# Grouped-query scores with the low part of the keys on both halves of the partitions

## The chip, the cores and the metric

The kernel runs on one core of a Trainium2 chip. The metric is the time of one execution on the device in microseconds (us), taken as the median of several runs. The engines that matter here are TensorE (PE in the rows; PEld is its weight load), VectorE (DVE), ScalarE (ACT) and GpSimd (POOL).

## The reference

Two transformer layers over 512 latent tokens and 256 context tokens, width 1024, then a third block of another kind. In each layer there is, between two feed-forward halves, a mix of three parts: neighbourhood attention, pooling, and grouped-query attention with 8 query heads over 2 key heads of width 64. The change is in the scores of the last one:

```python
def _gqa_attend(q, k, v):
    s = jnp.einsum('bqkgd,bskd->bkgqs', q, k, preferred_element_type=jnp.float32) * (q.shape[-1] ** -0.5)
    p = jax.nn.softmax(s, axis=-1).astype(v.dtype)
    return jnp.einsum('bkgqs,bskd->bqkgd', p, v)
```

The latent queries attend to all 768 keys in both layers; the context queries attend to the 256 context keys, in layer 0 alone.

## The kernel before

Products are made from split operands. A float32 value is kept as a high part in the short float format (F32R) and a low part, the rest. `mm3` (L279 to L284) adds three matmuls for each pair of blocks: high by high, high by low, low by high; most of the kernel's time is spent there.

Scores of the grouped queries are stacked instead. A head has 64 rows, half of the 128 partitions. `stack_q` (L557) puts the high part of one head's queries on one half and the low part on the other; GpSimd's DMA queue carries the low part across (L564, L565). `QS` holds eight such stacks. `KS` (L590) has three slots of 768 keys. Slots 0 and 1 hold the high part of key head 0 and 1, and `other_half` (L649 to L651) copies each to the other half of the partitions, so that one matmul of 128 rows gives high by high and low by high. Slot 2 holds the low parts, head 0 on the lower half and head 1 on the upper (L623), and a second matmul of 64 rows adds high by low.

`scores` (L567) makes these two matmuls (L571 and L572) for each PSUM bank. A latent task (`gqa_tasks`, L756) is 128 queries of two heads: for each head 512 and 256 keys, so four matmuls a head. There are 16 tasks in each layer. A context task (`ctx_tasks`, L785) has one bank of 256 keys for each head, two heads a task, eight such tasks in layer 0, and then four more for the other attention (L802).

A task runs through `soft` (L508): the maximum on VectorE (L513), the exponential on ScalarE (L515), the reciprocal and the scaling on VectorE (L502, L506). Then `pair_pv` (L477) transposes the probabilities three or four chunks at a time on TensorE (L487), evacuates each group to SBUF, three on ScalarE and one on VectorE in turn (L491, L493), and multiplies by the values (L497, a form of 128 rows by 64 columns). `pipeline` (L528) emits the scores of a task and its softmax ahead of the previous task's product. There are two PSUM buffers for scores and three for transposes. The order on each engine is then set before the launch by a planner that works with estimated times; each engine runs its queue in that order. When the last reader of `QS` and `KS` is done, their space goes to the values of the neighbourhood attention, which GpSimd's queue then loads (L709), followed there by the pooling.

The lines before the change:

```python
            self.nc.tensor.matmul(S[:, c:c + n], q, kl[0][:, k], start=True, stop=False)
            self.nc.tensor.matmul(S[:, c:c + n], q[h], kl[1][h, k], start=False, stop=True)
```

Of the kernel before, what the change touches and what calls it, by code (L numbers as in the profile page):

```python
# [10 lines left out]
F32 = mybir.dt.float32  # L11
# [17 lines left out]
# columns of the small-vector array  # L29
# [16 lines left out]
class Net:  # L46
# [9 lines left out]
    # ------------------------------------------------------------------ set-up  # L56
    def setup(self):
# [20 lines left out]
        # conditioning vectors as stationary operands, padded to 32 columns  # L78
# [6 lines left out]
        # column i of ones  # L85
# [11 lines left out]
    def weights(self, src, pool=None, ahead=AHEAD, eng=None):  # L97
        """A [128, 1024] piece of weights, split."""
        pool = pool or self.W
        with self.tc.high_priority(offset=ahead):  # L100
            raw = self.raw()
            self.nc.sync.dma_start(raw, src)
            W = tuple(pool.tile([128, 1024], F32R, name=f"w{x}", tag=f"w{x}", bufs=4 if pool is self.W else 2) for x in "hl")
            self.split(*W, raw, eng)
        return W

    def unit(self, src, pool=None):
        """256 columns of a weight, as (hi, lo) per 128 rows."""
        W = []
        for q in range(2):  # L110
            w = [x.rearrange("p (k c) -> p k c", k=4) for x in self.weights(src[:, 1024 * q:1024 * q + 1024], pool)]
            W += [tuple(x[:, k] for x in w) for k in range(4)]
        return W

    # ------------------------------------------------------------------ conditioning
    def ada(self, n):
        """Chunk n of the modulation: 0-17 for the two layers, 18-20 for the last block."""
# [10 lines left out]
        for k in range(KB):  # L128
            raw = self.fp.tile([128, 1024], F32, name="rawf", tag="rawf", bufs=self.nraw)
            nc.sync.dma_start(raw, src[:, k])  # L130
            if acc:
                # the sums over rows 128 apart on the vector engine, those over the partitions at the end
# [36 lines left out]
    def open_psum(self):  # L169
        """The PSUM banks of all phases but attention: transposes and sums, products, modulation."""  # L170
# [9 lines left out]
    def fill_chunk(self):  # L180
        """Finish the chunk that fill has begun, so that its PSUM bank is free."""
# [3 lines left out]
    def fill(self, n=1):  # L185
        """Emit n steps of the work that waits for nothing in the main chain."""
# [7 lines left out]
    # ------------------------------------------------------------------ norms  # L194
# [6 lines left out]
    def parts(self, ctx):  # L201
        """The pieces in which one phase hands the tokens over to the next: (column of the modulation, first, number)."""
# [13 lines left out]
    def rstd_rows(self, src, c0, n, eps):  # L216
        """PSUM bank with (mean(src)+eps)^-0.5 of each column, on all partitions."""
# [26 lines left out]
    def norm_mod(self, l, i, part):  # L244
        """aT = rmsnorm(h) * norm_g * (1 + scale) + shift of some tokens, split for the float32r products."""
# [19 lines left out]
    def defer(self, fn, depth=2):  # L265
        """Emit fn after the next depth deferred ones, so that the tensor engine has products to do until its input is there."""
# [12 lines left out]
    def mm3(self, ps, w, a, first, last):  # L279
        """ps += w^T a with both operands split in two parts."""  # L280
# [5 lines left out]
    # ------------------------------------------------------------------ feed-forward  # L286
    def ffn(self, l, i, up, down, ctx, hand_over, beside=None):
        """h += gate / 2 * swiglu(aT); hand_over(part) is called as soon as a part of h is final."""
# [8 lines left out]
        with ExitStack() as es:  # L297
# [48 lines left out]
            for n in splits[:-1]:  # L346
                us, wd = [], []
                for f in range(f0, f0 + n):
                    if f == 0 and not beside:
                        # the norm of the last part runs on beside the first two blocks of the others  # L350
# [11 lines left out]
                    # not at the ends, where the norms need the vector engine  # L362
# [11 lines left out]
                    if dp is not None:  # L374
                        if f < 2:
                            # the last of the norms comes first
# [20 lines left out]
    # ------------------------------------------------------------------ attention and pooling  # L397
    def na_bias_scratch(self, l):
        """The relative bias laid out by query column, row distance and key column, in DRAM."""
# [24 lines left out]
    def rope_tables(self, l):  # L424
        """[q, k] x token tile x [cos, +-sin] tables with the norm gain (and 1/8 for q) in them."""
# [16 lines left out]
    def head_norm(self, ps, nh, t, which, out):  # L442
        """out = rope(rmsnorm(ps) * g) for the heads of one token tile (no rotation for the context)."""
# [25 lines left out]
    def transpose_to(self, src, n, ev):  # L469
        """PE transposes of n chunks of 128 columns; ev takes the PSUM bank."""  # L470
# [6 lines left out]
    def pair_pv(self, P, n, v, o):  # L477
        """o = [V_a^T P_a^T; V_b^T P_b^T] of two heads, for n key chunks of 128."""
# [29 lines left out]
    def soft(self, S, n, act=False):  # L508
        """The softmax of the rows of S."""
# [9 lines left out]
    def follow(self, tasks, fn):  # L519
        """Let fn be called after the last of the tasks."""  # L520
# [7 lines left out]
    def pipeline(self, tasks, depth, beside=iter(()), steps=(), deep=None):  # L528
        """Each task is (scores, softmax, product, after): the scores and the softmax run ahead of the product.

        The scores of the tasks from deep on run two tasks ahead. beside is other work, in steps, for the tensor engine to
        do meanwhile.
        """
# [23 lines left out]
    def stack_q(self, dst, a, b, src):  # L557
        """Two heads on the two halves of the partitions: [hi; lo] stacks of the first (dst a) and [lo; hi] of the second."""
# [8 lines left out]
    def scores(self, S, q, ks, kl, h):  # L567
        """S[128 queries, keys] from stacked operands, in banks: (column, key slice) pairs."""
        for c, k in ks:
            n = k.stop - k.start  # L570
            self.nc.tensor.matmul(S[:, c:c + n], q, kl[0][:, k], start=True, stop=False)  # L571
            self.nc.tensor.matmul(S[:, c:c + n], q[h], kl[1][h, k], start=False, stop=True)  # L572

    def mix(self, l, qctx, hand_over):
# [5 lines left out]
        with ExitStack() as es, ExitStack() as fs, ExitStack() as rs:  # L580
# [9 lines left out]
            KS = qk.tile([128, 3, NT], F32R, name="KS")  # L590
            nc.gpsimd.memset(U, 0.0)
            with ExitStack() as ws:
# [20 lines left out]
                def ev_kv(t, p):  # L613
# [5 lines left out]
                    def ev(pt):  # L619
                        for b in range(2):  # L620
                            h = slice(64 * b, 64 * b + 64)
                            nc.scalar.activation(KS[h, b, ts], pt[h, :128], AF.Copy)
                            nc.vector.tensor_tensor(KS[h, 2, ts], pt[h, :128], KS[h, b, ts].bitcast(F32), OP.subtract)  # L623
# [25 lines left out]
                def other_half():  # L649
                    for b in range(2):  # L650
                        nc.gpsimd.dma_start(KS[64 - 64 * b:128 - 64 * b, b], KS[64 * b:64 * b + 64, b])  # L651
# [17 lines left out]
                def ev_u(b, p, nm, c0, n):  # L669
                    u0 = 8 if nm == "x" else 536  # L670
                    done = nc.scalar.activation(U[:, b, u0:u0 + n], p, AF.Copy)
                    if b == 0 and c0 == 0:
                        # the table of the exponential, ahead of the attention
# [8 lines left out]
            with ExitStack() as ats:  # L682
                self.ges.close()
                if not qctx:
                    # from here on token t = 4 i + r is at place 128 r + i
# [37 lines left out]
            # output projection: the first blocks of all tokens, then the last ones part after part  # L723
# [28 lines left out]
    def places(self, x, perm):  # L752
        """Columns in the order of the tokens when token 4 i + r is at place 128 r + i."""
        return x.rearrange("d (r i) -> d i r", r=4) if perm else x

    def gqa_tasks(self, QS, KS, vc, oT, perm):  # L756
        """Grouped-query attention of the latent tokens over all tokens, heads (i, 4 + i) at a time."""
        tasks = []
        for i in range(4):
            st = {}  # L760
            for t in range(4):
# [3 lines left out]
                def scores(i=i, ts=ts, d=d):  # L765
                    d["S"] = []
                    for b in range(2):
                        S = self.ps.tile([128, 1024], F32, name="S", tag="s")
                        self.scores(S, QS[:, 2 * i + b, ts], [(0, slice(0, 512)), (512, slice(512, NT))], (KS[:, b], KS[:, 2]),
                                    slice(64 * b, 64 * b + 64))  # L770
# [14 lines left out]
    def ctx_tasks(self, QS, KS, vc, qaT, kaT, va, oT):  # L785
        """Both attentions of the context over itself, two heads at a time."""
        mm = self.nc.tensor.matmul
        tasks = []
        for i in range(6):
            st = {}  # L790
            for t in range(2):
# [3 lines left out]
                def scores(i=i, ts=ts, d=d):  # L795
                    S = self.ps.tile([128, 1024], F32, name="S", tag="s")
                    for b in range(2):
                        r = slice(64 * b, 64 * b + 64)
                        if i < 4:
                            self.scores(S, QS[:, 2 * i + b, ts], [(512 * b, slice(NX, NT))], (KS[:, b], KS[:, 2]), r)  # L800
# [20 lines left out]
    def na_tasks(self, qaT, kaT, va, vj, nab, oT, perm):  # L821
        """Neighbourhood attention: 16 columns of all rows, two heads at a time."""
# [51 lines left out]
    def pool_mix(self, l, U, oT, qctx, ap):  # L874
        """Windowed means minus the input, a product per group, and the scale."""
# [28 lines left out]
    # ------------------------------------------------------------------ last block: Hyena filters  # L904
# [3 lines left out]
    def split_tables(self):  # L908
        """The cos and sin tables of both directions, split, to DRAM."""
# [9 lines left out]
    def dft_tables(self, pool, which):  # L919
        """cos and sin tables of one direction, split: [128, 2 (cos, sin), 1024] each."""  # L920
# [6 lines left out]
    def dft_forward(self, ps, tab, z, cs, par, kb):  # L927
        """ps = the cos or sin sums over the tokens of one parity, for 128 frequencies."""
# [4 lines left out]
    def sine(self, out, ps, b, f, pool):  # L933
        """out = sin(f * (ps + b)), the argument taken to [-pi, pi] first."""
# [11 lines left out]
    def filters(self):  # L946
        """Spectra of the two long filters, scaled for the inverse, to DRAM.

        The even part of a filter pair (forward + backward) gives the cosine sums, the odd part the sine sums.
        """  # L950
# [5 lines left out]
        with ExitStack() as es:  # L956
# [17 lines left out]
            # the backward filter has no tap at 0  # L974
# [4 lines left out]
            for cs in range(2):  # L979
# [5 lines left out]
                for hf in range(2):  # L985
# [3 lines left out]
                    for o in range(2):  # L989
# [7 lines left out]
                        for par in range(2):  # L997
# [6 lines left out]
                            if par == 0 and cs == 0:  # L1004
# [3 lines left out]
                                # frequency 256  # L1008
# [29 lines left out]
    # ------------------------------------------------------------------ last block  # L1038
# [3 lines left out]
    def b2_block(self, W, evs, cols=slice(0, NX)):  # L1042
        """The two feature-major blocks of a unit, each given to its ev."""
# [14 lines left out]
    def block2_norm(self, part):  # L1058
        """The final norm of h and the modulated layer norm of that, of the tokens at some places.

        h becomes hg = h * final_g less its mean; the final norm is r (h + mean) with r in rr[.., 0], r * mean in rr[.., 1].
        """
# [7 lines left out]
        # the mean of hg, on all partitions  # L1070
# [20 lines left out]
        # per token, tokens on partitions: the sum of h^2 and the mean of hg  # L1091
# [12 lines left out]
        # s = r (r^2 var + eps)^-0.5  # L1104
# [24 lines left out]
    def residual(self):  # L1129
        """The final norm of h times 2^(1/4), tokens on partitions, to DRAM."""  # L1130
# [139 lines left out]
    def b2_rattn(self, sr):  # L1270
        """sigmoid(r_attn); four of the blocks take the place of the queries and keys that are done."""
# [13 lines left out]
    def b2_merge_attn(self, sr):  # L1285
        """sigmoid(r_attn) * (y_attn @ w_proj_attn), to DRAM."""
# [12 lines left out]
    def proj(self, s, q):  # L1299
        """Four blocks of one of the two merge projections, split."""  # L1300
# [6 lines left out]
    def b2_hyena(self):  # L1307
        """Input projections of the Hyena branch and its two long convolutions; the gates fill the tensor engine meanwhile."""
# [316 lines left out]
def arrays_of(i):  # L1625
    c = np.ascontiguousarray
    A = {}
# [133 lines left out]
```

## Time and profile before

| what | value |
|---|---|
| median of 3 runs | 3518.68 us (3505.75 to 3519.12) |
| span of the profiled execution, first to last instruction | 3509.3 us |
| TensorE busy | 3429.8 us, 98% of the span |
| VectorE, ScalarE, GpSimd busy | 57%, 32%, 10% |
| granted TensorE clock, mean | 0.986 of full speed |
| latent scores and products, layer 0 | 786.9 to about 886 us |
| latent scores and products, layer 1 | 2270.8 to about 2376 us |

The profile gives the span of the profiled execution, not its time with what lies around it; the span is 9.4 us under the median of the runs. Times within the trace count from the first instruction. A matmul's end is modelled, and matmuls overlap, so the pace of TensorE is read from the starts of consecutive matmuls. [...]

### The profile page before, as it was taken

To read this page: it belongs to the slowest core of one execution; us is meant where nothing else is said; L and a number is where in the kernel's file an instruction comes from. 1 tells how busy PE (TensorE), PEld (TensorE's weight loads), DVE (VectorE), ACT (ScalarE), POOL (GpSimd) and SP (SyncE) were. 2 spreads that over 40 slices of the span, in tenths; PEclk is the share of its full clock that TensorE was granted. 3 is DMA by queue.
4 is the path that set the end of the run, shared out by engine and by line. 5 is a ranking of instruction groups with operands and counts; after the bars stand their busy time and mean duration, and the time that the engine had idled before them with its cause. 6 is when DMAs were issued, how large, how long until landed. Compare 5 with 4: busy or idle time off the path is not lost.

```text
span 3509.3 us, 51702 instructions
## 1 busy us (share of the span) xinstructions
PE 3429.8 (98%) x21236; PEld 2937.4 (84%) x21236; DVE 1990.6 (57%) x3373; ACT 1107.3 (32%) x2008; POOL 366.1 (10%) x432
## 2 busy tenths in 40 slices
PE   7999999999899999999999999999999999999997
PEld 5888889996599888899888889866888897777886
DVE  7535566835754566566455447467644463343687
ACT  4311112425632212223111123445422243344331
POOL 3300000231200000000000001512000010000134
PEclk9999999999999999999999999999999999999999
DMA  7533343131122344422344441302323223122344
GB/s 265 165 108 108 108 132 115 50 75 16 24 85 72 111 130 133 129 75 97 97 150 144 133 137 34 94 7 87 111 96 103 72 89 106 62 70 97 127 172 148
DMA packets 112861, 362.75 MB, mean 103 GB/s; under 512 B 15751, under 2 KB 25547, under 8 KB 111984
## 3 DMA queue, kind: packets, MB, share of 16 engines
q1 hardware_dynamic: 90208, 307.59, 27.0%
q0 software_dynamic: 22416, 51.85, 5.1%
q8 instruction: 167, 2.74, 0.3%
q14 instruction: 70, 0.57, 0.1%
HBM read 338.12 MB, written 19.31 MB: 102 GB/s over the span
## 4 chain that ended last, share of the span: by engine, by line
PE 67%; DVE 4%; ACT 1%; DMA 1%; issue 1%; POOL 0%; DVEq 0%; ACTq 0%; POOLq 0%
PE mm L282 16%; PE mm L283 16%; PE mm L284 16%; PE pw L282 3%; PE pw L283 3%; PE pw L284 3%; PE ops L497 2%; PE ptr L487 2%; PE S L572 1%; PE S L1236 1%; PE S L571 1%; DMA rawf<-in_w_ada 0%; DVE P L506 0%; DVE raw L1473 0%; DVE s L855 0%
## 5 line engine op out<-in xcount | busy, mean ns | idle before, releaser
L283 PE MATMUL mm<-aTl,wh 128*128 128x256 f32 (+1 forms) x2992 | 988.6, 331 | 0.0
L282 PE MATMUL mm<-aTh,wh 128*128 128x256 f32 (+1 forms) x2992 | 985.5, 331 | 2.3 <-ACT aTh L259 2.3
L284 PE MATMUL mm<-aTh,wl 128*128 128x256 f32 (+1 forms) x2992 | 986.8, 330 | 0.0
L283 PEld LDWEIGHTS mm<-aTl,wh 128*128 128x128 f32 x2992 | 569.3, 190 | 57.1 <-issue 4.1
L282 PEld LDWEIGHTS mm<-aTh,wh 128*128 128x128 f32 x2992 | 568.6, 191 | 56.7 <-ACT aTh L259 3.2
L284 PEld LDWEIGHTS mm<-aTh,wl 128*128 128x128 f32 x2992 | 569.6, 190 | 53.7 <-issue 2.9
L277 DVE TENSOR_TENSOR wl<-raw,wh 128x1024 fp32r<-128x1024 f32 x292 | 357.9, 1227 | 346.8 <-ACT wh L276 342.4
L276 ACT ACTIVATE wh<-raw 128x1024 fp32r<-128x1024 f32 x300 | 317.1, 1059 | 454.3 <-PE mm L283 287.4
L282 PE MATMUL mm<-uh,dh 128*128 128x256 f32 (+1 forms) x1368 | 449.8, 329 | 3.1 <-DVE h L340 1.9
L283 PE MATMUL mm<-ul,dh 128*128 128x256 f32 (+1 forms) x1368 | 448.3, 328 | 0.0
L284 PE MATMUL mm<-uh,dl 128*128 128x256 f32 (+1 forms) x1368 | 448.2, 328 | 0.0
L340 DVE SCALAR_TENSOR_TENSOR h<-mm,hg,h 128x256 f32<-128x256 f32 (+1 forms) x512 | 292.2, 582 | 174.9 <-PE mm L284 174.3
L319 DVE TENSOR_TENSOR sil<-sil,mm 128x256 f32<-128x256 f32 (+1 forms) x170 | 90.5, 533 | 342.6 <-PE mm L284 340.2
L282 PEld LDWEIGHTS mm<-uh,dh 128*128 128x128 f32 x1368 | 260.3, 190 | 28.0 <-DVE h L340 2.7
L283 PEld LDWEIGHTS mm<-ul,dh 128*128 128x128 f32 x1368 | 260.3, 190 | 22.8 <-issue 0.8
L284 PEld LDWEIGHTS mm<-uh,dl 128*128 128x128 f32 x1368 | 260.3, 190 | 22.7 <-issue 0.4
L135 DVE SCALAR_TENSOR_TENSOR acc<-rawf,cond,acc 128x1024 f32<-128x1024 f32 x189 | 236.0, 1281 | 72.4 <-DMA rawf<-in_w_ada 71.7
L276 ACT ACTIVATE dh<-rawf 128x1024 fp32r<-128x1024 f32 x88 | 92.0, 1058 | 489.1 <-DMA rawf<-in_ffn_down 376.1
L318 ACT ACTIVATE sil<-mm 128x256 f32<-128x256 f32 (+1 forms) x170 | 78.9, 464 | 457.9 <-PE mm L284 456.8
L277 DVE TENSOR_TENSOR dl<-rawf,dh 128x1024 fp32r<-128x1024 f32 x88 | 107.1, 1223 | 104.9 <-ACT dh L276 104.5
L282 PE MATMUL pw<-aTh,wh 128*128 128x512 f32 x400 | 158.6, 396 | 1.1 <-ACT x L1343 1.1
L283 PE MATMUL pw<-aTl,wh 128*128 128x512 f32 x400 | 157.9, 395 | 0.0
(389 smaller groups left out, 4994.5 us busy)
## 6 DMA issues: line engine op xcount, KB each, us to landing
raw<-in_ffn_up SPq DMA_DIRECT2D x176, 512.0 KB, 3.8
rawf<-in_w_ada SPq DMA_DIRECT2D x168, 512.0 KB, 4.4
raw<-in_w_in SPq DMA_DIRECT2D x100, 512.0 KB, 3.6
rawf<-in_ffn_down SPq DMA_DIRECT2D x88, 512.0 KB, 3.6
raw<-in_w_out SPq DMA_DIRECT2D x24, 512.0 KB, 5.4
Hs<-Hf POOLq DMA_DIRECT2D x16, 256.0 KB, 3.6
dft<-tab POOLq DMA_DIRECT2D x8, 512.0 KB, 6.2
raw<-in_w_proj SPq DMA_DIRECT2D x8, 512.0 KB, 3.7
```

The costliest lines, as they stand in the source:

```text
L135: nc.vector.scalar_tensor_tensor(acc[i], raw, self.cond[:, k, x:x + 1], acc[i], op0=OP.mult, op1=OP.add)
L276: self.hi = self.nc.scalar.activation(hi, src, AF.Copy)
L277: return (eng or self.nc.vector).tensor_tensor(lo, src, hi.bitcast(F32), OP.subtract)
L282: mm(ps, w[0], a[0], start=first, stop=False)
L283: mm(ps, w[0], a[1], start=False, stop=False)
L284: mm(ps, w[1], a[0], start=False, stop=last)
L318: nc.scalar.activation(s[:, :n], ps[0][:, :n], AF.Silu)
L319: nc.vector.tensor_tensor(s[:, :n], s[:, :n], ps[1][:, :n], OP.mult)
L340: nc.vector.scalar_tensor_tensor(self.h[:, j, c0:c0 + n], p[:, :n], hg[0][:, j, v:v + 1], self.h[:, j, c0:c0 + n], op0=OP.mult, op1=OP.add)
L487: nc.tensor.transpose(pt[:, 128 * c:128 * c + 128], P[b][:, 128 * (c0 + c):128 * (c0 + c) + 128], self.ident)
L497: nc.tensor.matmul(o[64 * b:64 * b + 64], v(b, c), PT[b][c], start=c == 0, stop=c == n - 1)
L571: self.nc.tensor.matmul(S[:, c:c + n], q, kl[0][:, k], start=True, stop=False)
```

## The change

`KS` gets a fourth slot. The low part of key head 1 goes to slot 3 instead of sharing slot 2, and `other_half` carries the slots b and 2 + b across together, so that each low part too stands on both halves. The second matmul of `scores` then takes the whole stacked query and all 128 rows, as the first does. It adds the product of both low parts, which was left out before. The number of matmuls, their columns and the number of transfers stay. Elsewhere the diff only removes comments.

```diff
-    def scores(self, S, q, ks, kl, h):
+    def scores(self, S, q, ks, kl):
         for c, k in ks:
             n = k.stop - k.start
-            self.nc.tensor.matmul(S[:, c:c + n], q, kl[0][:, k], start=True, stop=False)
-            self.nc.tensor.matmul(S[:, c:c + n], q[h], kl[1][h, k], start=False, stop=True)
+            for i, x in enumerate(kl):
+                self.nc.tensor.matmul(S[:, c:c + n], q, x[:, k], start=i == 0, stop=i == 1)
...
-            KS = qk.tile([128, 3, NT], F32R, name="KS")
+            KS = qk.tile([128, 4, NT], F32R, name="KS")
...
-                            nc.vector.tensor_tensor(KS[h, 2, ts], pt[h, :128], KS[h, b, ts].bitcast(F32), OP.subtract)
+                            nc.vector.tensor_tensor(KS[h, 2 + b, ts], pt[h, :128], KS[h, b, ts].bitcast(F32), OP.subtract)
...
-                        nc.gpsimd.dma_start(KS[64 - 64 * b:128 - 64 * b, b], KS[64 * b:64 * b + 64, b])
+                        nc.gpsimd.dma_start(KS[64 - 64 * b:128 - 64 * b, b::2], KS[64 * b:64 * b + 64, b::2])
...
-                        self.scores(S, QS[:, 2 * i + b, ts], [(0, slice(0, 512)), (512, slice(512, NT))], (KS[:, b], KS[:, 2]),
-                                    slice(64 * b, 64 * b + 64))
+                        self.scores(S, QS[:, 2 * i + b, ts], [(0, slice(0, 512)), (512, slice(512, NT))], (KS[:, b], KS[:, 2 + b]))
...
-                            self.scores(S, QS[:, 2 * i + b, ts], [(512 * b, slice(NX, NT))], (KS[:, b], KS[:, 2]), r)
+                            self.scores(S, QS[:, 2 * i + b, ts], [(512 * b, slice(NX, NT))], (KS[:, b], KS[:, 2 + b]))
```

## Rows read from the trace of the kernel before

**Rows 1.** The page: span, part 1, and a weight load of part 5 (busy, mean ns).

```profile
span 3509.3 us, 51702 instructions
PE 3429.8 (98%) x21236; PEld 2937.4 (84%) x21236; DVE 1990.6 (57%) x3373; ACT 1107.3 (32%) x2008; POOL 366.1 (10%) x432
...
L284 PEld LDWEIGHTS mm<-aTh,wl 128*128 128x128 f32 x2992 | 569.6, 190 | 53.7 <-issue 2.9
```

**Rows 2.** Windows: stretch, length, busy PE, PEld, DVE, ACT, POOL, clock, DMA, GB/s.

```profile
786.90:886.00 99.10, 98.44 (x611) 63.02 (x609) 59.27 (x108) 49.62 (x106) 19.07 (x27) 0.93 0.11 17
886.00:922.00 36.00, 34.28 (x250) 22.16 (x249) 23.86 (x75) 24.49 (x79) 8.97 (x11) 1.00 0.18 36
...
2270.80:2376.00 105.20, 104.60 (x639) 65.59 (x637) 64.01 (x111) 53.85 (x112) 21.10 (x29) 0.94 0.08 16
```

**Rows 3.** Chain of waits, layer 1, 2291 to 2382 us: share by line.

```profile
by line: PE ops L497 30.1%; PE ptr L487 28.4%; PE S L572 21.1%; PE S L571 18.4%; PE S L838 1.4%; PE S L841 0.9%
```

**Rows 4.** TensorE timeline (start us, duration us, engine, line, shape): plain products.

```profile
783.73 0.39 PE L283 MATMUL mm<-aTl,wh 128*128 128x512 f32 x1
783.96 0.39 PE L284 MATMUL mm<-aTh,wl 128*128 128x512 f32 x1
...
785.13 0.28 PE L284 MATMUL mm<-aTh,wl 128*128 128x256 f32 x1
785.25 0.28 PE L282 MATMUL mm<-aTh,wh 128*128 128x256 f32 x1
```

**Rows 5.** TensorE timeline, layer 1: two heads of scores, then a product.

```profile
2344.00 0.49 PE L571 MATMUL S<-KS,QS 128*128 128x512 f32 x1
2344.43 0.50 PE L572 MATMUL S<-KS,QS 64*128 64x512 f32 x1
2344.86 0.38 PE L571 MATMUL S<-KS,QS 128*128 128x256 f32 x1
2345.17 0.38 PE L572 MATMUL S<-KS,QS 64*128 64x256 f32 x1
2345.48 0.49 PE L571 MATMUL S<-KS,QS 128*128 128x512 f32 x1
...
2346.96 0.33 PE L497 MATMUL ops<-PT,vc 128*64 128x128 f32 x2
```

**Rows 6.** TensorE timeline, layer 0 at half clock: a head's scores begin and end.

```profile
796.55 0.78 PE L571 MATMUL S<-KS,QS 128*128 128x512 f32 x1
...
799.00 0.90 PE L487 MATMUL ptr<-ident,P 128*128 128x128 f32 x3
```

**Rows 7.** The tile S: first scores line, ns min/median/max, first and last start, forms.

```profile
L571 PE MATMUL S<-KS,QS x144: 362/387/796, 787.1 to 2372.7; 128*128 128x256 f32 x80, 128*128 128x512 f32 x64
```

**Rows 8.** Timeline of all engines, layer 1: between two groups of transposes.

```profile
2337.13 0.55 PE L487 MATMUL ptr<-ident,P 128*128 128x128 f32 x3
...
2337.71 0.56 DVE L493 COPY PT<-ptr 128x384 f32<-128x384 f32 x1 [0.86 <-PE ptr L487]
...
2338.19 0.61 DVE L506 TENSOR_SCALAR P<-P,rs 128x768 f32<-128x768 f32 x1
...
2338.89 0.33 PE L487 MATMUL ptr<-ident,P 128*128 128x128 f32 x1
```

**Rows 9.** TensorE timeline, opening of layer 0: idle time before it, and releaser.

```profile
790.63 0.50 PE L571 MATMUL S<-KS,QS 128*128 128x512 f32 x1 [0.66 <-ACT P L515]
```

**Rows 10.** Windows: four latent tasks of layer 0.

```profile
846.60:872.90 26.30, 26.30 (x177) 16.77 (x176) 15.86 (x30) 13.51 (x29) 0.00 (x0) 1.00 0.00 1
```

**Rows 11.** GpSimd's timeline, and the line L651: the key copies and their landing.

```profile
695.11 1.15 POOL L651 DMA_DIRECT2D KS<-KS  x2
...
DMA to landing us min/median/max: 2.6/3.5/5.2
```

**Rows 12.** Windows of 5 us: where the granted clock fell.

```profile
831.00:836.00 5.00, 5.00 (x22) 3.13 (x23) 2.61 (x4) 1.88 (x4) 0.00 (x0) 0.69 0.00 0
...
2385.00:2390.00 5.00, 2.08 (x26) 1.63 (x26) 4.96 (x9) 0.19 (x1) 4.83 (x4) 0.93 0.55 164
```

## The prediction, made before the change was run

> **What bounds the kernel now.** I read the page first: TensorE is busy over 98% of the span, every other engine far less [rows 1]. That is an average, so I went to the two stretches the change touches, by windows. The grouped-query scores run in layer 0 from 786.9 us (latent queries to about 886, context queries to about 906) and in layer 1 from 2270.8 to about 2376. In both TensorE is marked busy without a hole worth the name (98.44 of 99.10 us, 104.60 of 105.20), VectorE and ScalarE are busy about 60% and 50% [rows 2]. The chain of waits agrees for layer 1: from 2291 to 2382 it never leaves TensorE, and 39.5% of it is the two scores lines, L571 and L572 [rows 3]. For layer 0 the printed chain breaks off at 925.7 us, so there the windows must do.
>
> Busy does not mean streaming. In the TensorE timeline look at distances from start to start, not at durations. Plain products, 128 rows on 128 rows, follow each other every 0.23 us with 512 columns and every 0.12 us with 256, and each has its own weight load of 190 ns, fully hidden [rows 1, 4]. The scores of one head (512 and 256 keys, two matmuls each) should take 0.23 + 0.23 + 0.12 + 0.12 = 0.70 us at that pace. They take 1.48: 0.43, 0.43, 0.31 and 0.31 [rows 5]. Each of the four matmuls thus carries some 0.19 to 0.20 us in which nothing streams. What separates them from the products is that L571 has 128 rows, L572 has 64, and they alternate.
>
> **The change, part by part.** *The second matmul.* L572 keeps its columns and its count and gets 128 rows and the same stationary operand as L571. The four matmuls of a head then look like four plain products into the same bank, so I cost them at 0.70 us: 0.78 saved per head. One edge remains: a head followed by a probabilities-times-values matmul (128 by 64) still changes form. Today such a head also takes 1.48, to 2346.96 [rows 5], its last step 0.31; I leave that step as it is, so such a head saves 0.19 less, 0.59. In four tasks of layer 1 (2330.5 to 2356.9) there are eight heads, six followed by a transpose or by scores, two by a product (one of them shown [rows 5]). That is 6 x 0.78 + 2 x 0.59 = 5.9 us per four tasks; both layers have 16 tasks, eight such groups: 47 us. Four heads fall into half-clock stretches, where a head takes 2.45 us [rows 6] and would take twice 0.70: 0.27 more each, 1 us. The context queries of layer 0 have 16 pairs of 256 keys (the scores lines have 80 pairs of 256 in all [rows 7], 64 of them latent), each 0.62 now and 0.24 then, 6 us; their share of softmax work is larger (VectorE and ScalarE busy two thirds of that stretch [rows 2]), so I count 4.
>
> [...]
>
> *What comes back as waits.* A freed TensorE waits where the scores hide something. In a stretch of layer 1 [rows 8] a transpose group starts at 2337.13; VectorE must copy its result (2337.71, 0.56 us) before it scales the next probabilities (2338.19, 0.61), which the next transposes need at 2338.89. The cover is exactly one head's scores. With those at 0.70 instead of 1.46 the transposes wait for the rest, and the head's whole 0.76 comes back. The four tasks from 2330.5 have this sequence twice, here and at their start; those are the two tight places; the other heads stand ahead of work whose scaling ended earlier. 2 x 0.76 x 8 = 12 us. Then the opening of each stage: the second task's scores wait already today for the first exponential (0.66 us [rows 9]); with two score banks and TensorE done sooner, about two heads' savings are lost there, 1.5 us per layer, 3 us.
>
> Could VectorE or ScalarE become the bound outright? In a 26.3 us window of four tasks they are busy 15.86 and 13.51 us [rows 10], 3.97 and 3.38 per task; a task takes 6.58 now and 5.1 if all is saved. Neither is the bound by volume, though VectorE would be at 78%, so waits for order (as at 2338.89 [rows 8]) are what counts.
>
> *The wider key copy.* Line L651's transfers now carry the low part too, twice the 192 KB, and wait for the last L623 on VectorE instead of L622 on ScalarE. They are issued at 695 us and land in 2.6 to 5.2 us [rows 11]; the first reader is at 786.9, so even a tripled landing is hidden: 0. On GpSimd's queue the rotation adds (L467) of the queries stand behind them; a wait of under 2 us and perhaps another 0.6 us per issue delays transposes that are deferred by two token tiles behind products; 0, and at most 2 us if that cover fails. The extra 3 KB per partition and the changed index of L623 cost no time that a row shows. L709 (values) starts when the last reader of QS and KS is done, so it and the pooling on GpSimd move earlier with the scores; what follows the stage shifts as a block.
>
> **The sum.** 47 + 1 + 4 - 12 - 3 = 37 us. The page's span is 3509.3; 3472.3 after. The median of the runs, 3518.68, lies 9.4 us above that span (3505.75 to 3519.12, so the profile resembles the slower two); I carry the 9.4 over: 3481.7, called 3482.
>
> **Rivals.** *All of it arrives.* If the order tolerates the waits, or the scores hold the clock up better, nothing of the 15 us comes back: 52, and up to 10 more if half-clock stretches shrink: 3457 to 3467. For it: the clock fell to 0.69 in a window of 831 to 836 with TensorE marked busy throughout [rows 12], just behind two heads of scores in a row, which would stream twice as densely. Against: the stage opens with idle TensorE anyway, more than now. Chance 0.18.
>
> *The softmax chain takes over.* If five of eight heads turn out tight instead of two, 5 x 0.76 x 8 = 30 us return, and 52 - 30 - 3 leaves about 19: 3500. For it: VectorE works in order, and every copy waits for a transpose. Against: its volume. Chance 0.13.
>
> *Nothing goes away.* The step of 0.43 and 0.31 is also 190 ns of load plus 0.23 or 0.12 of streaming [rows 1, 4, 5]. If it is a load that isn't hidden because both matmuls write one bank or because of the stacked operand, not because of the rows, the new pair costs the same: 3518. Against it: the products accumulate in one bank too. Chance 0.05.
>
> *Slower: the clock.* TensorE with holes can fall to half clock: at 2385 to 2390 it was busy 2.08 of 5 us, and the granted clock fell there (0.93 in that window) [rows 12]. A task's 5.1 us of TensorE work would become 10.2, against 5.4 forecast: 4.8 us lost per task. The gain of 37 is used up when 8 of the 32 tasks run at half clock beyond those that do today; with 13 of them the time is 13 x 4.8 - 37 = 25 us longer, 3544. Against: at 85% and more TensorE would be far busier than in that window. Chance 0.05.
>
> **How the numbers follow.** Forecast 3482 (gain 27 to 47) 0.59; the rivals as above. My range takes in all of the full gain and the tight chain: 3454 to 3506; outside are the last two rivals and the edges. Faster by over 0.5% (17.6 us, below 3501; about what a measurement of this kernel can tell from no change): 0.59 + 0.18 + half of 0.13 = 0.84. Same: the other half and the third rival, 0.11. Slower: 0.05.
>
> **What would show it.** After: the scores of a head at full clock start to start 0.23, 0.23, 0.12, 0.12 (if 0.43 and 0.31 stay, the drain was something else); the latent stages shorter by about 15 to 17 us in layer 0 and as much in layer 1; TensorE in them with holes released by L506 (scaling) and L515 (exponential), together some 7 us per layer; granted clock of these stages no lower than 0.93. If the transposes wait at most heads, not a quarter of them, the softmax chain has taken over; if the stage runs long at 0.5, the last.

## The result and the profile after

The changed kernel takes 3456.53 us in the median (3456.12 to 3457.64), the kernel before 3516.45 (3505.75 to 3519.12, one more run than above): a ratio of 0.9836, 95% interval 0.9821 to 0.9852. The gain is 60 us where 37 were forecast. In the changed kernel the two scores matmuls are one line, L575, and the key copy is L654.

The page, with the lines that answer to [rows 1]:

```profile
span 3454.3 us, 51702 instructions
PE 3363.5 (97%) x21236; PEld 2919.2 (85%) x21236; DVE 1991.2 (58%) x3373; ACT 1105.6 (32%) x2008; POOL 369.2 (11%) x432
```

The span is 55.0 us shorter with the same number of instructions, and only TensorE, with its weight load, is less busy by more than 2 us. Of the 55.0, 29.6 lie between the first and the last grouped scores of layer 0 (125.0 us before, 95.4 after) and 27.1 between those of layer 1 (102.1 and 75.0). Everything else together is 1.7 us longer. The profiled execution took 3456.12 us, 1.8 us more than its span.

Windows of both kernels (stretch, its length, busy time of PE, PEld, DVE, ACT and POOL, granted clock, DMA share, GB/s). Before, the grouped scores of layer 0 and of layer 1:

```profile
787.00:912.00 125.00, 124.23 (x791) 80.15 (x790) 74.78 (x157) 66.19 (x157) 18.97 (x27) 0.95 0.09 14
2270.90:2373.00 102.10, 101.50 (x610) 63.37 (x608) 62.36 (x108) 51.67 (x108) 20.35 (x28) 0.93 0.08 17
```

After, the same two stages, then four latent tasks, which answer to [rows 10]:

```profile
787.00:882.40 95.40, 91.91 (x791) 72.26 (x790) 75.40 (x157) 64.65 (x156) 20.46 (x27) 1.00 0.08 18
2244.70:2319.70 75.00, 72.47 (x611) 57.07 (x609) 61.48 (x108) 50.73 (x107) 21.56 (x28) 1.00 0.10 23
839.20:860.00 20.80, 20.80 (x178) 16.19 (x177) 15.68 (x31) 13.51 (x31) 0.00 (x0) 1.00 0.01 2
```

Two things to see. Four tasks take 20.8 us, not 26.3, and TensorE is still busy without a hole in them, with VectorE now at 75%. And the clock of both stages is 1.00, where it was 0.95 and 0.93.

Over both stages TensorE now sits idle for 6.0 us, where it was 1.4. These five places hold 4.5 of them; the brackets give the idle time before the matmul and what ended it:

```profile
789.98 1.85 PE L575 MATMUL S<-KS,QS 128*128 128x512 f32 x8 [1.44 <-ACT P L515]
805.09 0.52 PE L487 MATMUL ptr<-ident,P 128*128 128x128 f32 x3 [0.80 <-DVE P L506]
877.22 0.41 PE L487 MATMUL ptr<-ident,P 128*128 128x128 f32 x2 [0.37 <-DVE P L506]
2247.59 1.85 PE L575 MATMUL S<-KS,QS 128*128 128x512 f32 x8 [1.38 <-ACT P L515]
2267.22 0.52 PE L487 MATMUL ptr<-ident,P 128*128 128x128 f32 x3 [0.55 <-DVE P L506]
```

TensorE and its neighbours after, layer 1, at a place with the same order of work as [rows 8], one turn of four tasks later (start, duration, engine, line, shape; x4 are four matmuls in a row, 512, 512, 256 and 256 columns):

```profile
2312.92 0.55 PE L487 MATMUL ptr<-ident,P 128*128 128x128 f32 x3
...
2313.22 0.95 PE L575 MATMUL S<-KS,QS 128*128 128x512 f32 x4
2313.50 0.56 DVE L493 COPY PT<-ptr 128x384 f32<-128x384 f32 x1 [0.71 <-PE ptr L487]
...
2313.98 0.61 DVE L506 TENSOR_SCALAR P<-P,rs 128x768 f32<-128x768 f32 x1
2314.00 0.49 PE L487 MATMUL ptr<-ident,P 128*128 128x128 f32 x3
```

A head's scores run from 2313.22 to 2314.00: 0.78 us where 1.46 to 1.48 stood [rows 5, 8]. And the transposes at 2314.00 start while the scaling that the prediction put ahead of them has just begun (2313.98 to 2314.59), and before the copy has ended (2314.06). They need neither.

The openings, 15 us from the first scores, layer 0 and layer 1; first the kernel before, then the changed one:

```profile
787.00:802.00 15.00, 14.34 (x49) 8.65 (x49) 8.73 (x16) 6.59 (x14) 11.52 (x23) 0.66 0.72 105
2270.90:2285.90 15.00, 14.40 (x39) 7.87 (x37) 8.11 (x14) 7.21 (x15) 12.59 (x24) 0.69 0.53 106
```

```profile
787.00:802.00 15.00, 13.52 (x104) 10.61 (x104) 11.73 (x22) 10.28 (x23) 12.31 (x23) 1.00 0.50 107
2244.70:2259.70 15.00, 13.59 (x105) 10.71 (x105) 11.82 (x23) 11.02 (x24) 13.35 (x24) 1.00 0.48 107
```

TensorE has more idle time in the openings than before, as expected, and still the granted clock is 1.00 in both. Before, the clock was 0.50 from 791.9 to 802.1 us in layer 0 and from 2276.7 to 2290.3 in layer 1, and TensorE did less than half as many matmuls in the same 15 us (49 and 39; now 104 and 105).

### The profile page after: what moved, and what is told of

Read it like the earlier page. It is cut to its first block, busy times and chain, and to the rows that moved or that the text cites. A ratio compares the mean times of both kernels' runs of the same rounds, so it can differ in the third digit from the quotient of the medians.

```text
span 3454.3 us, 51702 instructions
## 1 busy us (share of the span) xinstructions
PE 3363.5 (97%) x21236; PEld 2919.2 (85%) x21236; DVE 1991.2 (58%) x3373; ACT 1105.6 (32%) x2008; POOL 369.2 (11%) x432
## 4 chain that ended last, share of the span: by engine, by line
PE 89%; DVE 5%; issue 2%; DMA 1%; ACT 1%; POOL 1%; DVEq 0%; ACTq 0%; POOLq 0%
PE mm L283 23%; PE mm L282 23%; PE mm L284 23%; PE pw L282 3%; PE pw L283 3%; PE pw L284 3%; PE ops L497 3%; PE ptr L487 2%; PE S L575 1%; DVE P L506 1%; PE S L1238 1%; DMA rawf<-in_w_ada 1%; DVE nm L513 0%; PE pad L150 0%; PE pad L142 0%
```

## The experiments

A form is the rows by columns of the array that a matmul takes, such as 128 by 128 or 64 by 128. Theory: what goes away is the change of form between a 128-row and a 64-row matmul, and with it the half clock of the openings. Rivals: the new layout or the planner's new order brings the gain; a 64-row matmul is slow in itself, or the weight load is exposed; and, for what the prediction got wrong, the waits behind VectorE's copy. All times are medians beside runs of the kernel before on the same chip.

**The layout alone** (e1_layout).

```diff
+            KS = qk.tile([128, 4, NT], F32R, name="KS")
+                        nc.gpsimd.dma_start(KS[64 - 64 * b:128 - 64 * b, b::2], KS[64 * b:64 * b + 64, b::2])
...
             self.nc.tensor.matmul(S[:, c:c + n], q[h], kl[1][h, k], start=False, stop=True)
```

> Four key slots and the wider copy as in the change, but the second scores matmul still on 64 rows (q[h] against KS[h, 2 + b]). Theory (what the change saves is the step between a 128-row and a 64-row matmul): as before, 3516 us within 6, a head's steps stay 0.43, 0.43, 0.31, 0.31 us, and the openings of both stages still fall to half clock. Rival (the new layout, the copy or the order that the planner makes of it bring the gain): near 3456 us. If the wider copy costs anything, it shows here as time above 3519 us.

3513.61 us, ratio 0.9999 (0.9989 to 1.0008). The wider copy, the wait for VectorE's L623 and the fourth slot cost nothing and bring nothing. In the changed kernel the copies land in 3.7 to 6.8 us (2.6 to 5.2 before [rows 11]), over 80 us ahead of their first reader in layer 0. The openings are at half clock here too (0.68 and 0.77, below).

**Half as many changes of form** (e2_grouped).

```diff
         for c, k in ks:
-            n = k.stop - k.start
-            self.nc.tensor.matmul(S[:, c:c + n], q, kl[0][:, k], start=True, stop=False)
-            self.nc.tensor.matmul(S[:, c:c + n], q[h], kl[1][h, k], start=False, stop=True)
+            self.nc.tensor.matmul(S[:, c:c + k.stop - k.start], q, kl[0][:, k], start=True, stop=False)
+        for c, k in ks:
+            self.nc.tensor.matmul(S[:, c:c + k.stop - k.start], q[h], kl[1][h, k], start=False, stop=True)
```

> Kernel before with three slots, but in a latent head both banks' 128-row matmuls come first and both banks' 64-row matmuls after them, so the form changes twice in a head instead of four times. Theory (a form change costs 0.19 us): steps 0.23, 0.31, 0.23, 0.31, a head 1.08 instead of 1.48 us, 64 heads save 26 us: 3490 us, and less if the clock dips of the openings shorten. Rival (each matmul exposes its weight load of 0.19 us, whatever stands beside it): steps stay 0.43, 0.31, 0.43, 0.31, 3516 us.

3480.46 us, ratio 0.9904 (0.9889 to 0.9919): 34 us less with the same matmuls, loads and columns in another order. TensorE's timeline of one head and the transposes after it:

```profile
834.18 0.60 PE L570 MATMUL S<-KS,QS 128*128 128x512 f32 x2
834.71 0.61 PE L572 MATMUL S<-KS,QS 64*128 64x512 f32 x2
835.25 0.55 PE L487 MATMUL ptr<-ident,P 128*128 128x128 f32 x3
```

0.53 + 0.54 = 1.07 us a head, as expected from two changes of form instead of four. An exposed weight load beside every matmul would have left 1.48. The gain is 8 us larger than the 26 expected from the form alone; the half-clock stretches of the openings are shorter here too, 3.4 us each where they were 10.2 and 13.7.

**64 rows throughout** (e3_rows64).

```diff
-            self.nc.tensor.matmul(S[:, c:c + n], q, kl[0][:, k], start=True, stop=False)
+            self.nc.tensor.matmul(S[:, c:c + n], q[h], kl[0][h, k], start=True, stop=False)
```

> Both scores matmuls on 64 rows: the first takes q[h] and the high part on the same half, so the product of the queries' low part with the keys' high part is left out. Columns and number of matmuls stay. Theory (form change): within a head the steps are 0.23, 0.23, 0.12, and the change of form is paid on entry and on exit, 0.19 each: about 1.08 us a head, 3490 us. Rival (64-row matmuls are slow in themselves, or the load is exposed): steps 0.43 and 0.31 as before, 3516 us. Whether the openings still fall to half clock tells if the density of columns or the rows in use go with the clock.

3467.75 us, ratio 0.9865 (0.9849 to 0.9882). One head of this kernel on TensorE, and the next transposes; after them two heads in a row:

```profile
829.91 0.50 PE L571 MATMUL S<-KS,QS 64*128 64x512 f32 x1
830.25 0.39 PE L572 MATMUL S<-KS,QS 64*128 64x512 f32 x1
830.48 0.28 PE L571 MATMUL S<-KS,QS 64*128 64x256 f32 x1
830.60 0.28 PE L572 MATMUL S<-KS,QS 64*128 64x256 f32 x1
830.81 0.87 PE L487 MATMUL ptr<-ident,P 128*128 128x128 f32 x6
...
838.88 0.51 PE L571 MATMUL S<-KS,QS 64*128 64x512 f32 x2
839.23 0.40 PE L572 MATMUL S<-KS,QS 64*128 64x512 f32 x2
839.47 0.28 PE L571 MATMUL S<-KS,QS 64*128 64x256 f32 x2
839.58 0.28 PE L572 MATMUL S<-KS,QS 64*128 64x256 f32 x2
839.79 0.44 PE L487 MATMUL ptr<-ident,P 128*128 128x128 f32 x2
```

Between matmuls of one form the steps are 0.23 and 0.12 us, with 64 rows as with 128; L572 is as quick as a plain product [rows 4]. A 64-row matmul is not slow in itself. The time is 22 us below the expectation; part of the reason is in the last lines: two heads in a row, on opposite halves of the rows, take 0.91 us together, as long as one alone.

**The new form in the first four tasks only** (e4_first), **and in all but these** (e5_rest). The line is that of `gqa_tasks`, with four slots in both; in e5_rest the test is reversed and the context tasks have the new form.

```diff
-                                    slice(64 * b, 64 * b + 64))
+                                    slice(0, 128) if i == 0 else slice(64 * b, 64 * b + 64))
```

> Four slots; the new 128-row second matmul only in the first four latent tasks of each layer, the old form in all others. If the clock has no part in the gain: 8 tasks by 1.4 us, 11 us: 3505 us. If the half-clock stretches of the openings (10.2 and 13.7 us long in the kernel before) came from the sparse scores there, they go too, and with them 9 us more: 3496 us, with no half clock between 787 and 800 us or in the first 15 us of layer 1's scores.

> The reverse of e4_first: old form in the first four latent tasks of each layer, new form in all others and in the context tasks. If the clock of the openings hangs on the scores there, the half-clock stretches stay, and the time is 3456 + 11 + 9: 3476 us. If it doesn't, 3456 + 11: 3467 us.

e4_first takes 3491.88 us, ratio 0.9935 (0.9920 to 0.9950): 23 us less, where eight tasks without the clock would give 11. e5_rest takes 3473.34 us, ratio 0.9888 (0.9869 to 0.9906): 41 us less. The two sum to 64 us, against 54 to 60 for the whole change. The openings (windows as above) of e1_layout, e4_first and e5_rest, in this order:

```profile
787.60:802.60 15.00, 14.34 (x52) 8.93 (x51) 8.90 (x16) 6.60 (x14) 12.15 (x23) 0.68 0.56 105
2273.60:2288.60 15.00, 14.40 (x50) 8.08 (x49) 8.89 (x15) 7.33 (x15) 12.62 (x24) 0.77 0.49 107
```

```profile
787.50:802.50 15.00, 13.53 (x103) 10.70 (x101) 11.73 (x22) 10.23 (x23) 12.49 (x23) 1.00 0.47 107
2263.10:2278.10 15.00, 13.60 (x103) 10.69 (x103) 11.78 (x23) 11.01 (x24) 13.36 (x24) 1.00 0.45 107
```

```profile
787.70:802.70 15.00, 14.34 (x50) 8.98 (x50) 8.94 (x16) 6.59 (x14) 11.59 (x23) 0.67 0.66 105
2250.70:2265.70 15.00, 14.40 (x61) 8.42 (x61) 9.81 (x17) 8.12 (x17) 12.44 (x24) 0.89 0.50 107
```

With the new form in the opening the clock stays at 1.00 in both layers; with the old form there it falls, whatever the later tasks do. How far it falls in layer 1 varies (0.69, 0.77, 0.89).

**Half the rows in the opening, the columns as dense** (e8_first64), beside **the change again** (a2_change).

```diff
+                                    slice(64 * b, 64 * b + 64) if i == 0 else None)
...
+            self.nc.tensor.matmul(S[:, c:c + n], q[h], kl[0][h, k], start=True, stop=False)
+            self.nc.tensor.matmul(S[:, c:c + n], q[h], kl[1][h, k], start=False, stop=True)
```

> The change itself once more, beside the three others of this call: 3456 us within 4, ratio to before near 0.984.

> The changed kernel, but in the first four latent tasks of each layer both scores matmuls on 64 rows (the queries' low part left out there): columns as dense as in the change, but half the rows. By form changes alone (0.30 us a head, 16 heads): 5 us slower than a2_change, 3461 us. If the half-clock stretches of the openings hang on the 64-row scores, as e3_rows64 (10.2 and 13.7 us at half clock) against e4_first (none) suggests, they come back and cost some 10 us more: 3471 us.

a2_change takes 3457.21 us, ratio 0.9845 (0.9828 to 0.9862). e8_first64 takes 3461.60, 4.4 us more. Its openings:

```profile
787.50:802.50 15.00, 12.88 (x56) 9.56 (x56) 9.96 (x19) 7.75 (x17) 12.55 (x23) 0.60 0.43 107
2249.50:2264.50 15.00, 12.84 (x63) 9.21 (x64) 10.43 (x19) 8.99 (x19) 13.50 (x24) 0.68 0.44 107
```

The half clock is back in both layers, though here no form changes inside a head. The time alone would have said that it costs nothing; the trace says otherwise. The first three task periods take 17.3 and 16.2 us where the change takes 10.9 and 10.8, of which 6 heads by 0.30 us are form. The later tasks, in another order of the planner, took 1.9 and 4.6 us less than in the change and hid part of it. So that the clock falls is shown; its price is not given by this run. Nor does it part the rows from the changes of form: a head here has none inside, but still changes between 64 rows and the 128 of the transposes at its ends.

**VectorE's copy of the transposed probabilities** (e6_evac, and again as e9_evac beside a2_change), on top of the change.

```diff
-                self.evac = "aaav"
+                self.evac = "a"
```

> The changed kernel, with all groups of transposed probabilities of the latent tasks evacuated by ScalarE (evac 'a' for 'aaav'). The prediction held that VectorE's copy ahead of the scaling makes the transposes wait at two of eight heads, 0.76 us each, 12 us in all. If that is so, these waits go: 3445 us. Rival (the transposes that follow there don't need that scaling): the copy was off the path, 3456 us within 4, or slower if ScalarE, then at about 3.9 of 5.2 us a task, delays the products.

> The kernel of e6_evac again, on the same chip as the change. If the small gain of 3.6 us seen between separate calls is real, this is 3 to 5 us under a2_change; if it was the difference of two chips, the two are equal within 2 us.

3452.68 us, and 3449.71 beside 3457.21 for the change: 4 to 7.5 us faster, not 12. Where both ran on one chip, all runs of e9_evac (3446.41 to 3450.71) lie under all of the change (3454.54 to 3457.61). Four tasks of e9_evac:

```profile
838.00:857.80 19.80, 19.80 (x178) 15.78 (x177) 14.16 (x26) 14.26 (x34) 0.00 (x0) 1.00 0.01 2
```

19.8 us instead of 20.8, and TensorE without a hole in either: what went away was not a wait that the trace shows on TensorE. Its timeline counts 18 changes of form in these four tasks (scores and transposes 128 by 128, products 128 by 64) instead of 22 in the changed kernel. If these changes cost as much as those of the scores (0.15 to 0.2 us, below), four fewer are 0.6 to 0.8 of the 1.0 us; that was not tested by itself. e9_evac is the fastest kernel here that computes everything: 0.9822 (0.9807 to 0.9836) of the kernel before.

**What sets the pace after the change** (e7_onepass).

```diff
-            self.nc.tensor.matmul(S[:, c:c + n], q, kl[0][:, k], start=True, stop=False)
-            self.nc.tensor.matmul(S[:, c:c + n], q, kl[1][:, k], start=False, stop=True)
+            self.nc.tensor.matmul(S[:, c:c + n], q, kl[0][:, k], start=True, stop=True)
```

> The changed kernel without the second scores matmul: the products with the keys' low part are left out. 64 heads lose 0.23 + 0.12 us and 16 context pairs 0.12: 24 us of TensorE work. If TensorE still sets the pace of the changed stages: 3456 - 24 = 3432 us, and a latent task falls from 5.2 to about 4.5 us. If the softmax chain (VectorE, ScalarE) has become the bound, as in the rival of the prediction: 3450 us or more, with TensorE idle behind L506 and L515.

3433.82 us, ratio 0.9777 (0.9759 to 0.9795): 23.4 us under a2_change, where 24 us of TensorE work left. For these 24 us TensorE still sets the pace after the change: its idle time in the two stages grew only from 6.0 to 9.6 us. VectorE is then busy 87% and 89% of the two stages.

## Why the prediction was right, and where its sizes were off

**Right.** The bound, the mechanism and the direction. The stage was bound by TensorE; nearly 0.2 us went with each change of form (a head with four of them fell from 1.48 to 0.78 us); the copy cost nothing (e1_layout); the rival of the exposed load fell (e2_grouped, 1.07 us a head where it asked for 1.48); and the planner's order is not the gain, for TensorE runs the same sequence of matmuls before and after in the whole stage of layer 0, and in layer 1 from the eighth task on. The context tasks gave 4 us, as forecast: the stretch from the last latent task's scores to the last grouped scores of layer 0 went from 28.1 to 22.4 us, of which about 1.4 is that latent task's own. "The drain" in the prediction's last paragraph is the author's word for the 0.19 to 0.20 us in each scores matmul; the traces show the steps, not what TensorE does in them.

The forecast itself was 25 us too slow, and 3456.5 lies 2.5 us inside the lower end of the range: the range held because it took in the first rival, not because the sum was right.

**The waits that did not come back: 9 us.** The forecast took 47 us for the time lost at changes of form and gave 12 back to waits behind VectorE's scaling. Measured, four steady tasks went from 26.4 to 20.8 us, 5.6; times eight that would be 45 us, and 44 arrived (the 56.7 of both stages less 4.3 for the context and 8.1 for the openings, below). Behind the scaling TensorE waited 1.7 us in all, at the three places shown, none of them in the steady tasks. The step that failed is the reading of [rows 8]: that the transposes at 2338.89 "need" the scaling that ended just before. Two groups of transposes go with one head and one scaling. Counted from the start of the layer, those at 2338.89 are group 36 and read head 18; the scaling at 2338.19 is number 20. Number 18 had ended 6.7 us before them:

```profile
2331.55 0.61 DVE L506 TENSOR_SCALAR P<-P,rs 128x768 f32<-128x768 f32 x1
```

The same count gives the scaling that had just ended at 805.09 and 2267.22, where the trace names L506 as the releaser. That number 20 ended 0.09 us before 2338.89 was chance of the schedule; one turn later, after the change, such transposes start 0.02 us after such a scaling begins. e6_evac and e9_evac show 4 to 7.5 us for the whole copy, with TensorE full in both.

**The head's own saving was slightly less:** a head takes 0.78 us (2313.22 to 2314.00 above), not 0.70; its first step is 0.31 us where 0.23 was forecast, for a reason not tested. In four tasks the scores gave 5.3 us (from 11.8 to 6.5) and the transposes behind them 0.3, 5.6 where 5.9 were forecast.

**The openings: 10 us.** The forecast gave them +1 for heads at half clock and -3 for waits on the exponential. Measured, the first three periods went from 18.0 to 10.9 us in layer 0 and from 20.2 to 10.8 in layer 1, 16.5 us; three tasks by 1.40 us in each layer account for 8.4. The other 8.1 came with the half clock's going. The prediction had that as a rival's extra, "up to 10 more if half-clock stretches shrink", and argued against it that the opening would have more idle TensorE than now. It has (13.52 of 15 us busy, 14.34 before), and the clock held. e4_first and e8_first64 show what went with it: 128-row scores in the opening 1.00, 64-row scores, alone or alternating, 0.60 to 0.89. Waits on the exponential did come, about half of the 3 us: TensorE waited 1.44 and 1.38 us, where it waited 0.66 and 0.60 before.

**The carried 9.4 us.** Around the span lie 1.8 us (3456.12 against 3454.3; 3511.79 against 3510.0 for e1_layout), so the profiled execution of before took about 3511, a little under its median, not 3519. The forecast span was 3472.3; against the measured 3454.3 the miss is 18 us: 9 from the waits, 10 from the openings, 0.3 from the context, less 1.7 elsewhere. What happened is the first rival, to which the prediction gave 0.18: all of it arrives, and the half-clock stretches go; it stood at 3457 to 3467.

**The slower rival** had the sign of the clock's answer wrong: it made TensorE's holes the risk and left out what ran between them. In the window that it named, the clock was 0.50 from 2389.3 us on, in a gap of 2.48 us without a matmul. In the two stages the holes grew from 1.4 to 6.0 us, and the clock rose from 0.95 and 0.93 to 1.00.

## What to carry to other kernels

Read TensorE's pace from start to start and compare it with the same shape elsewhere in the trace: a short matmul that alternates with a full-height one can cost more than its columns (here 0.43 us for 512 columns that take 0.23 in a plain product), and filling the idle rows with a harmless product may be free (here a head fell from 1.48 to 0.78 us). Before a saving is given back to a wait, find out what the waiting instruction reads: a releaser in its row names it, and where the engine was not idle and the row names none, counting the instructions of both lines does. Two instructions that follow each other closely are no dependency by that alone. And when a stage opens at half clock, try what the matmuls of its first tasks look like before blaming its gaps.

## What the runs showed of the hardware

The changes between 128-row and 64-row matmuls cost TensorE on average 0.15 to 0.2 us each: with four of them a head takes 1.48 us [rows 5] and with none 0.78 (the change), both at a granted clock of 1.00, and with two 1.07 (e2_grouped). A weight load of the changed scores takes 0.19 us (L575, median of 288). Four of these exposed would have left a head at some 0.70 + 4 x 0.19 = 1.46 us, an estimate from these loads and the pace of the plain products [rows 4]; four full-height matmuls with their loads took 0.78.

Not expected: the granted clock of an opening went with the rows of its scores. In ten openings with both scores matmuls on 128 rows (the change in both its profiles, e4_first, e6_evac, e9_evac) it was 1.00; in the twelve with 64-row scores among them or alone (before, e1_layout, e2_grouped, e3_rows64, e5_rest, e8_first64) it was 0.60 to 0.89. Before, e1_layout and e5_rest had TensorE busy longer than the change in that stretch (14.34 to 14.40 us of 15, the change 13.52 to 13.59), e3_rows64 and e8_first64 less long (12.84 to 12.94). It is no rule of the rows alone: e7_onepass, with half the scores matmuls and all on 128 rows, held 1.00 in layer 0 and fell in layer 1 for 3.4 us (0.89 over the first 15). And 64-row scores always brought changes of form at the ends of a head, so no run here tells the rows from these. What the clock costs was not measured by itself; the traces put both openings at some 8 us, e4_first (23 us where 11 were due to the form) at some 11. And 64-row matmuls of two heads on opposite halves ran side by side, 0.91 us for both heads.
